# When a neighbourhood head transposes its probabilities and values: one step one half tile later, two steps one or two half tiles sooner

## The chip, the core and the metric

One core of a Trainium2 chip runs the whole program in one launch. The metric is the device time of one execution in microseconds (us). The engines are TensorE (PE in the profile; PEld is its weight load), VectorE (DVE), ScalarE (ACT), GpSimd (POOL) and SyncE (SP, which issues the transfers). The accumulators of TensorE lie in a memory of its own with eight banks, which VectorE and ScalarE read.

## The reference

Two layers of an encoder trunk work on 512 grid tokens (8 rows of 64) and 16 meta tokens, with a model width of 1024, all in float32. In each layer one projection feeds two attention branches: grouped-query attention over all tokens, and neighbourhood attention, in which a grid token sees a window of 8 rows by 16 columns with a learned bias, and the meta tokens. Cut to what matters here:

```
proj = rms_norm(x) @ w_in            # qa ka va za | qb kb vb zb | ga gb
oa   = gqa_attention(qa, ka, va) * silu(za)          # 8 heads of 64, 2 key heads
# neighbourhood attention, 8 heads of 64:
s_win  = qb . kb[window] + bias ;  s_meta = qb . kb[meta]
p      = softmax(concat(s_win, s_meta))
ob     = (p_win . vb[window] + p_meta . vb[meta]) * silu(zb)
x      = x + (sigmoid(ga) * (oa @ w_o_attn) + sigmoid(gb) * (ob @ w_o_na)) @ w_out
```

## The kernel before

**The projection is the backbone.** The input projection runs in chunks of 128 output columns, named in `project`. Each float32 product is three matmuls on two-part operands: high by high (L266), low by high (L267), high by low (L268). After about 12 matmuls over 512 tokens, or 24 over 264, `product` calls `tick()`. One such stretch is a **half tile**, about 2.9 us of TensorE's time. The weights come in 128x512 pieces: a raw transfer (`raw`), a cast by ScalarE (`whi`, L214) and a subtract by GpSimd (`wlo`, L216).

**Side work is put between the half tiles.** Both attention branches are cut into steps. A `Side` queue starts a new unit every four ticks, and each step runs a fixed number of ticks after its unit's start, as tables say: `GQA_AT` for the grouped-query units (`scores` S, transposes `pt`, meta transposes `ptm`, sums `av`), `NA_AT` for the neighbourhood heads. The two queues have starting ticks 0 and 1 of four. At one tick, the neighbourhood steps go first; the steps of the queue due at that tick go in the order of their start, a new unit last.

**A neighbourhood head** has six steps, placed by `stages`: `prepare` (loads the bias), `scores` (the score tile `Sb`, eight matmuls; VectorE adds the bias and finds the maximum, L733; ScalarE takes exponentials, L735; VectorE normalises them into `Pb`, L739), and three groups of transposes of `Pb`: `transposes1` (`ta`, and `tm` for the meta queries in layer 0), `transposes2` (`tb`), `transposes3` (`tc`); then `sums` (`avb`). `values` places three more groups for each pair of heads, which transpose the values: `vtb`, `vtc`, `vtd`, for the tile `VB2`.

**Emptying a bank.** Every transposed group goes into a bank of one pool (`ps_t`, tag `tp`) that has two banks; the next but one group needs the bank empty. ScalarE copies the high part and VectorE subtracts for the low part (`split`, L172 and L173; `split_down`, L609 and L610). The group `tb` has four such ops: two for its 128 rows, two for its 64. The score tiles `S` and `Sb` share one buffer of two banks, and the exponentials of S (`P`, L624) read it.

**Numbers used in the prediction.** A half tile is numbered by the tick count modulo 4. Heads 0 to 7 start at ticks that are 1 modulo 4, so step offset 2 is half tile 3, offset 4 is half tile 1 and offset 5 is half tile 2. The functions that the diff touches:

Of the kernel before, what the change touches and what calls it, by code (L numbers as in the profile page):

```python
# [33 lines left out]

GQA_AT = ({"scores": (0, 2), "transposes": (3, 4), "meta": 5, "sums": (5, 7)},
          {"scores": (0, 1), "transposes": (3, 6), "meta": 6, "sums": (5, 7)})
NA_AT = ({"stages": (0, 2, 5, 5, 5, 7), "values": (3, 4, 6)},
         {"stages": (0, 2, 4, 5, 5, 7), "values": (3, 4, 5)})

NORM_AT = ({"tokens": (1, 4, 6), "squares": (2, 2, 2, 3, 2), "heads": (2, 3, 5, 5, 6), "values": (1, 3)},  # L40
           {"tokens": (1, 3, 5), "squares": (2, 2, 2, 3, 2), "heads": (2, 3, 5, 5, 6), "values": (1, 3)})
# [50 lines left out]
def trunk_kernel(ctx: ExitStack, tc: tile.TileContext, xT, w, gn, bias, rope, outT):  # L92
# [255 lines left out]
    for l in range(DEPTH):  # L348
# [474 lines left out]
        def window_values(j, i):  # L823
            vb = kvq[j]["v"]
            if i == 0:
                kvq[j]["v2"] = tiny.tile([P, 6, 2, 2, HD], F32R, tag="VB2", bufs=1, name=f"VB2{l}_{j}")
                kvq[j]["o"] = slot("B", f"ob{l}_{j}")
            tiles = ([(1, 64, P), (2, 192, P), (3, 320, P)], [(4, 0, 64), (5, 448, 64)], [(0, NTOK - 32, 32)])[i]
            values(vb, kvq[j]["v2"], tiles, f"{'bcd'[i]}{l}_{j}")

        def start_head(hd):
            steps = list(zip(NA_AT[l]["stages"], windowed_head(hd)))
            if hd % 2 == 0:
                steps += [(at, lambda i=i: window_values(hd // 2, i)) for i, at in enumerate(NA_AT[l]["values"])]
            return sorted(steps, key=lambda x: x[0])
# [178 lines left out]
```

## Time and profile before

| what | value |
|---|---|
| three runs | 889.19, 889.79, 890.23 us; median 889.79 |
| the profiled execution | 890.2 us, its span 888.4 us, granted clock 0.993 |
| TensorE busy | 863.5 us, 97% of the span |
| VectorE, ScalarE, GpSimd busy | 561.6, 470.9, 356.5 us |
| neighbourhood heads of layer 0 | in the stretch 88 to 262 us |
| neighbourhood heads of layer 1 | in the stretch 517 to 700 us |

The profile is of one execution. A row of the timeline gives the start, the length, engine, line and operation, the output and inputs by the program's names, and in brackets how long the engine stood idle before it and what ended that. Matmuls overlap in these rows, so starts tell more than lengths. A row of the waits gives who waited for whom: total in us, how many times, the longest.

### The profile page before, as it was taken

Reading aid. Unit: us, or ns where it says so; the run is one execution under the profiler, and the core shown is the slowest. Engines: PE = TensorE matmul, PEld = TensorE weight load, DVE = VectorE, ACT = ScalarE, POOL = GpSimd, SP = SyncE. Lnnn points to the kernel's source line nnn. Section 1 sums busy time; section 2 is a strip of 40 time slices with the busy share of each in tenths; the row PEclk is TensorE's granted clock in tenths of the full one; section 3 lists DMA queues with packets and bytes.
Section 4 is the critical chain, followed back from the end, with each engine's and each line's share of the span. In section 5 each row is a group of like instructions: output and inputs, shape, how many; then the busy total and the mean of one; then the engine's idle time right before and its main releaser. Section 6 shows DMA issues by size and latency. Waiting matters only on the chain.

```text
span 888.4 us, 16647 instructions
## 1 busy us (share of the span) xinstructions
PE 863.5 (97%) x6208; PEld 806.4 (91%) x6208; DVE 561.6 (63%) x1285; ACT 470.9 (53%) x1045; POOL 356.5 (40%) x288
## 2 busy tenths in 40 slices
PE   8999999999999999999999999999999999999996
PEld 7988999999999999999998889988888888888896
DVE  6983777676876574336338657778867655444643
ACT  7732566666665554433445446566657554444532
POOL 5563433433223332544765544334333333345520
PEclk9998999999999999999999999999999999999998
DMA  8453343435222212324544454244421122222702
GB/s 274 114 149 100 102 126 89 128 95 134 80 73 67 66 60 84 96 84 156 185 135 125 127 161 127 78 113 137 124 79 62 59 73 72 72 83 95 262 21 76
DMA packets 51937, 96.46 MB, mean 109 GB/s; under 512 B 6544, under 2 KB 8592, under 8 KB 51856
## 3 DMA queue, kind: packets, MB, share of 16 engines
q1 hardware_dynamic: 50624, 94.33, 35.6%
q8 instruction: 49, 0.80, 0.4%
q10 hardware_dynamic: 1232, 1.06, 0.4%
q14 instruction: 32, 0.26, 0.1%
HBM read 76.20 MB, written 4.26 MB: 91 GB/s over the span
## 4 chain that ended last, share of the span: by engine, by line
PE 84%; DVE 8%; ACT 3%; DMA 2%; issue 1%; SPq 0%; POOL 0%; DVEq 0%; ACTq 0%; POOLq 0%
PE pp L266 19%; PE pp L268 19%; PE pp L267 19%; PE av L664 3%; PE pt L116 3%; PE y L266 3%; PE y L267 3%; PE y L268 3%; PE avb L797 2%; PE S L441 1%; PE S L442 1%; DVE Pb L739 1%; PE Sb L441 1%; DMA raw<-in_w_dram 1%; PE ptm L116 1%
## 5 line engine op out<-in xcount | busy, mean ns | idle before, releaser
L216 POOL TENSOR_TENSOR wlo<-raw,whi 128x512 fp32r<-128x512 f32 x216 | 290.3, 1348 | 433.7 <-ACT whi L214 384.7
L266 PE MATMUL pp<-hh,whi 128*128 128x264 f32 (+1 forms) x1056 | 335.4, 318 | 2.3 <-ACT qs L377 2.3
L268 PE MATMUL pp<-hh,wlo 128*128 128x264 f32 (+1 forms) x1056 | 330.2, 313 | 0.0
L267 PE MATMUL pp<-hl,whi 128*128 128x264 f32 (+1 forms) x1056 | 329.4, 312 | 0.0
L214 ACT CAST whi<-raw 128x512 fp32r<-128x512 f32 x216 | 132.9, 620 | 160.0 <-PE pp L267 54.5
L266 PEld LDWEIGHTS pp<-hh,whi 128*128 128x128 f32 x1056 | 199.7, 189 | 11.6 <-ACT qs L377 2.5
L268 PEld LDWEIGHTS pp<-hh,wlo 128*128 128x128 f32 x1056 | 199.9, 189 | 10.7
L267 PEld LDWEIGHTS pp<-hl,whi 128*128 128x128 f32 x1056 | 200.3, 190 | 8.9
L624 ACT ACTIVATE P<-S,st,r 128x528 f32<-128x528 f32 x64 | 50.6, 791 | 55.1 <-DVE st L623 49.4
L622 DVE TENSOR_REDUCE st<-S 128x1 f32<-128x528 f32 x64 | 45.0, 703 | 12.3 <-PE S L442 11.5
L173 DVE TENSOR_TENSOR ptl<-pt,pth 128x512 fp32r<-128x512 f32 x64 | 43.9, 687 | 13.6 <-ACT pth L172 13.1
L865 DVE TENSOR_TENSOR mg<-pp,rbc 128x264 f32<-128x264 f32 (+1 forms) x48 | 24.8, 517 | 41.6 <-PE pp L268 40.5
L172 ACT CAST pth<-pt 128x512 fp32r<-128x512 f32 x64 | 37.3, 585 | 9.7 <-PE pt L116 8.8
L116 PE MATMUL pt<-ident,P 128*128 128x128 f32 x256 | 39.5, 274 | 1.8 <-DVE VB L173 0.6
L626 DVE RECIPROCAL st<-st 128x1 f32<-128x1 f32 x64 | 10.5, 164 | 45.9 <-ACT P L624 45.4
L735 ACT ACTIVATE Pb<-Pb,stb 128x208 f32<-128x208 f32 (+1 forms) x64 | 31.0, 485 | 12.6 <-DVE stb L733 12.5
L267 PE MATMUL pp<-mxl,whi 128*128 128x264 f32 x128 | 36.7, 286 | 0.0
L268 PE MATMUL pp<-mxh,wlo 128*128 128x264 f32 x128 | 36.5, 285 | 0.0
L266 PE MATMUL pp<-mxh,whi 128*128 128x264 f32 x128 | 36.4, 285 | 0.0
L866 ACT ACTIVATE mg<-mg 128x264 f32<-128x264 f32 (+1 forms) x48 | 23.7, 493 | 22.3 <-DVE mg L865 22.1
L664 PE MATMUL av<-pth,VA 128*128 128x256 f32 x128 | 35.1, 296 | 0.0
L627 DVE TENSOR_SCALAR P<-P,st 128x528 f32<-128x528 f32 x64 | 33.6, 526 | 2.2
(616 smaller groups left out, 1848.6 us busy)
## 6 DMA issues: line engine op xcount, KB each, us to landing
raw<-in_w_dram SPq DMA_DIRECT2D x232, 256.0 KB, 2.7
bias<-in_bias_dram SPq DMA_DIRECT2D x16, 480.0 KB, 3.9
x<-in_xT_dram SPq DMA_DIRECT2D x8, 264.0 KB, 5.8
xr<-in_xT_dram SPq DMA_DIRECT2D x8, 264.0 KB, 4.5
x1d<-xr SPq DMA_DIRECT2D x8, 264.0 KB, 3.4
xf<-x1d SPq DMA_DIRECT2D x8, 256.0 KB, 5.3
KB_0l<-kb SPq DMA_DIRECT2D x8, 140.0 KB, 2.4
KB_1l<-kb SPq DMA_DIRECT2D x8, 140.0 KB, 2.4
```

The costliest lines, as they stand in the source:

```text
L116: nc.tensor.transpose(ps, src, ident[:n, :n])
L172: nc.scalar.copy(hi, src)
L173: split_at["any"] = nc.vector.tensor_sub(lo, src, hi.bitcast(F32))
L214: split_at["weights"] = nc.scalar.copy(hi, raw)
L216: sub = eng.tensor_sub(lo, raw, hi.bitcast(F32))
L266: nc.tensor.matmul(ps, wh, rh[:, a:b], start=i == 0, stop=False)
L267: nc.tensor.matmul(ps, wh, rl[:, a:b], start=False, stop=False)
L268: nc.tensor.matmul(ps, wl, rh[:, a:b], start=False, stop=i == n - 1)
L622: nc.vector.tensor_reduce(st[:n, 0:1], S[:n, :, :HALF], axis=AX.XY, op=ALU.max, negate=True)
L624: nc.scalar.activation(p[:n].rearrange("p (i k) -> p i k", i=2), S[:n, :, :HALF], AF.Exp, bias=st[:n, 1:2], scale=scale, accum_out=st[:n, ...
L627: nc.vector.tensor_scalar_mul(p[:n], p[:n], st[:n, 3:4])
L664: nc.tensor.matmul(c["av"], rows2(c["t"][i][0]), c["t"][i][1], start=i == 0, stop=i == 8)
```

## The change

Four entries of the table that places the steps of the neighbourhood heads are other numbers. In `stages` the fourth entry (`tb`) goes from 5 to 6 in both layers' terms, that is from half tile 2 to half tile 3, where the next head's `Sb` follows it. In `values` `vtd` of layer 0 goes from offset 6 to 4, and in layer 1 `vtc` from 4 to 3 and `vtd` from 5 to 4. No instruction is added or taken away, and no matmul has another shape.

```
-NA_AT = ({"stages": (0, 2, 5, 5, 5, 7), "values": (3, 4, 6)},
-         {"stages": (0, 2, 4, 5, 5, 7), "values": (3, 4, 5)})
+NA_AT = ({"stages": (0, 2, 5, 6, 5, 7), "values": (3, 4, 4)},
+         {"stages": (0, 2, 4, 6, 5, 7), "values": (3, 3, 4)})
```

In these listings a row is the line, the operation, the output and the inputs with their buffer numbers, and the shape; `ident` is the identity for a transpose and `pp` is the projection.

TensorE, layer 1, head 3. Before, `tb` and `tc` stand together at the end of a projection chunk:

```order
L268 MATMUL pp_24_0_8231<-hh_7_6415,wlo_24_1_8073 128x512
L116 MATMUL tb_3_8288<-ident,Pb_3_1_8105 128x128 x2
L116 MATMUL tb_3_8288<-ident,Pb_3_0_8104 64x128
L116 MATMUL tb_3_8288<-ident,Pb_3_1_8105 64x128
L116 MATMUL tc_3_8299<-ident,Pb_3_0_8104 32x128 x2
L116 MATMUL tc_3_8299<-ident,Pb_3_1_8105 32x128 x2
L664 MATMUL av_2_0_8306<-pth_2_0_0_8213,VA_6850 128x256
```

After, `tc` stands there alone, and `tb` comes half a tile later:

```order
L268 MATMUL pp_8_0_8327<-hh_3_6123,wlo_8_0_8222 128x512
L116 MATMUL tb_3_8340<-ident,Pb_3_1_8105 128x128 x2
L116 MATMUL tb_3_8340<-ident,Pb_3_0_8104 64x128
L116 MATMUL tb_3_8340<-ident,Pb_3_1_8105 64x128
L441 MATMUL Sb_4_8351<-KB_2h_8167,QB_2a 128x208
L442 MATMUL Sb_4_8351<-KB_2l_8174,QB_2a 128x208
```

`tb` of head 3 has moved from ahead of `tc` to directly ahead of the `Sb` of head 4.

ScalarE at the same place, before (the half tile's weight cast first):

```order
L214 CAST whi_17_1_8334<-raw_17_1_8332 128x512
L172 CAST tbh_3_8293<-tb_3_8288 128x256
L609 CAST na_120<-tc_3_8299 32x512
L586 ACTIVATE zb_2t<-zb_2_8217 128x512
L609 CAST tbh_3_8293<-tb_3_8288 64x256
L624 ACTIVATE P_2_1_1_8317,st_2_1_1_8316<-S_2_1_1_8311,st_2_1_1_8316,r_1_6912 128x528
L214 CAST whi_13_0_8454<-raw_13_0_8452 128x512
L735 ACTIVATE Pb_4_0_8353,stb_4_8352<-Pb_4_0_8353,stb_4_8352 128x208
```

And after:

```order
L214 CAST whi_17_1_8323<-raw_17_1_8321 128x512
L609 CAST na_120<-tc_3_8288 32x512
L586 ACTIVATE zb_2t<-zb_2_8217 128x512
L624 ACTIVATE P_2_1_1_8306,st_2_1_1_8305<-S_2_1_1_8300,st_2_1_1_8305,r_1_6912 128x528
L214 CAST whi_13_0_8460<-raw_13_0_8458 128x512
L172 CAST tbh_3_8345<-tb_3_8340 128x256
L609 CAST tbh_3_8345<-tb_3_8340 64x256
L735 ACTIVATE Pb_4_0_8353,stb_4_8352<-Pb_4_0_8353,stb_4_8352 128x208
```

The copies of `tb` have moved from ahead of the exponentials `P` to behind them and behind the next weight cast, directly ahead of head 4's first exponential.

VectorE at the same place, before:

```order
L173 TENSOR_TENSOR tbl_3_8294<-tb_3_8288,tbh_3_8293 128x256
L610 TENSOR_TENSOR na_120<-tc_3_8299,na_120 32x512
L622 TENSOR_REDUCE st_2_1_1_8316<-S_2_1_1_8311 128x1
L610 TENSOR_TENSOR tbh_3_8293<-tb_3_8288,tbh_3_8293 64x256
L623 TENSOR_SCALAR st_2_1_1_8316<-st_2_1_1_8316,r_1_6912 128x1
L587 SCALAR_TENSOR_TENSOR zb_2_8217<-zb_2t,zb_2_8217 128x512
```

And after:

```order
L610 TENSOR_TENSOR na_120<-tc_3_8288,na_120 32x512
L622 TENSOR_REDUCE st_2_1_1_8305<-S_2_1_1_8300 128x1
L587 SCALAR_TENSOR_TENSOR zb_2_8217<-zb_2t,zb_2_8217 128x512
L623 TENSOR_SCALAR st_2_1_1_8305<-st_2_1_1_8305,r_1_6912 128x1
L626 RECIPROCAL st_2_1_1_8305<-st_2_1_1_8305 128x1
L627 TENSOR_SCALAR P_2_1_1_8306<-P_2_1_1_8306,st_2_1_1_8305 128x528
L173 TENSOR_TENSOR tbl_3_8346<-tb_3_8340,tbh_3_8345 128x256
L610 TENSOR_TENSOR tbh_3_8345<-tb_3_8340,tbh_3_8345 64x256
L733 ISA Pb_4_0_8353,stb_4_8352<-Sb_4_8351,bias_4_8260 128x208
```

Both subtracts of `tb` have left the chain of the maximum (L622, L623) that `P` needs and stand ahead of head 4's score ops (L733); a gate multiply (L587) now stands ahead of L623.

TensorE, layer 1, head 2, before:

```order
L116 MATMUL ta_2_7979<-ident,Pb_2_0_7860 128x128 x3
L116 MATMUL ta_2_7979<-ident,Pb_2_1_7861 128x128
L565 MATMUL vtc_1_7988<-ident,vb_1_7524 64x128 x2
L441 MATMUL S_2_0_0_7996<-KA1h_7003,Q_1a 128x264
L442 MATMUL S_2_0_0_7996<-KA1l_7004,Q_1a 128x264
```

And after, where `vtc` stands one half tile ahead of this, directly behind `vtb`:

```order
L116 MATMUL ta_2_7985<-ident,Pb_2_0_7860 128x128 x3
L116 MATMUL ta_2_7985<-ident,Pb_2_1_7861 128x128
L565 MATMUL vtd_1_7994<-ident,vb_1_7524 32x128
L441 MATMUL S_2_0_0_8003<-KA1h_7003,Q_1a 128x264
L442 MATMUL S_2_0_0_8003<-KA1l_7004,Q_1a 128x264
```

`vtd` has taken the place of `vtc`; before it stood behind the next half tile's `tc`.

## Prediction

> **What bounds the kernel now.** I read the page first: busy times, slices, chain. Then TensorE's waits in the two stretches where neighbourhood heads run, and last the rows around each wait.
>
> ```profile
> span 888.4 us, 16647 instructions
> PE 863.5 (97%) x6208; PEld 806.4 (91%) x6208; DVE 561.6 (63%) x1285; ACT 470.9 (53%) x1045; POOL 356.5 (40%) x288
> PEclk9998999999999999999999999999999999999998
> ```
>
> TensorE is the bound: 97% busy at a nearly full clock. The change adds no matmul, so the time can move only through TensorE's gaps, 24.9 us in all (888.4 - 863.5). The next view gives the two stretches with heads (layer 0, layer 1) on TensorE: length, then busy time.
>
> ```profile
> 88.00:262.00 174.00, 171.29 (x1411) 166.95 (x1411) 126.17 (x380) 110.97 (x289) 60.94 (x51) 1.00 0.38 106
> 517.00:700.00 183.00, 179.61 (x1158) 158.93 (x1157) 136.96 (x336) 113.04 (x266) 64.51 (x55) 1.00 0.35 102
> ```
>
> Here the gaps are 2.71 us and 3.39 us. TensorE's waits, first in layer 0 and then in layer 1 (total, times, longest):
>
> ```profile
> PE tc L116 <- DVE tal L173: 1.1, 1, 1.1
> PE pt L116 <- DVE VB L173: 0.6, 1, 0.6
> PE pt L116 <- DVE st L623: 0.5, 1, 0.5
> ...
> PE vtd L565 <- DVE na L610: 1.4, 3, 0.8
> PE Sb L441 <- ACT P L624: 1.2, 3, 0.7
> PE vtc L565 <- DVE ptl L173: 0.5, 1, 0.5
> ```
>
> Most are of one kind: a transpose (tc, vtd, vtc, pt) waits for VectorE to finish reading what stands in its bank, since all transposes share two banks. `Sb` waits for the exponentials `P`, which read the one score tile.
>
> **The change: what it removes.** These are the waits one by one, with two neighbouring matmuls for scale (177.24, 177.36: start, length).
>
> ```profile
> 177.24 0.28 PE L266 MATMUL pp<-hh,whi 128*128 128x264 f32 x1
> 177.36 0.28 PE L267 MATMUL pp<-hl,whi 128*128 128x264 f32 x1
> 222.19 0.61 PE L116 MATMUL tc<-ident,Pb 128*32 128x128 f32 x4 [1.12 <-DVE tal L173]
> 539.30 0.29 PE L565 MATMUL vtd<-ident,vb 128*32 128x128 f32 x1 [0.24 <-DVE na L610]
> 584.93 0.41 PE L565 MATMUL vtc<-ident,vb 128*64 128x128 f32 x2 [0.53 <-DVE ptl L173]
> 591.81 0.29 PE L565 MATMUL vtd<-ident,vb 128*32 128x128 f32 x1 [0.78 <-DVE na L610]
> 613.10 0.36 PE L441 MATMUL Sb<-KB_2h,QB_2a 128*128 128x208 f32 x1 [0.74 <-ACT P L624]
> 630.26 0.28 PE L565 MATMUL vtd<-ident,vb 128*32 128x128 f32 x1 [0.38 <-DVE na L610]
> 683.89 0.37 PE L441 MATMUL Sb<-KB_3h,QB_3b 128*128 128x208 f32 x1 [0.17 <-ACT P L624]
> ```
>
> Matmuls start 0.12 us apart and last 0.28, so 0.16 of each lies over the next. A wait therefore costs its shown idle time plus 0.16.
>
> - Layer 0, head 5: `tc` came third in half tile 2, into the bank of `ta`, whose low part was late. Now `tc` comes second, into the bank of `tm`, which two short VectorE ops empty. Removed: 1.12 + 0.16 = 1.28 us.
> - Layer 1, the `vtd` behind `tc`: it moves one half tile ahead, to where `ta` stands, and `tb` no longer competes there. Removed: 0.40 + 0.94 + 0.54 = 1.88 us.
> - Layer 1, head 2: `vtc` goes directly behind `vtb` and takes the other bank. Removed: 0.53 + 0.16 = 0.69 us.
> - Layer 1, `Sb` at 613.10 and 683.89: 0.74 + 0.16 = 0.90 and 0.17; the second follows transposes, so I take it as shown. Both VectorE ops on `tb` stood among the steps that `P` waits for; they go. What is left of it is counted below as added, so gross 1.07 us.
>
> Gross removed: 1.28 + 1.88 + 0.69 + 1.07 = 4.9 us.
>
> **What it adds, layer 0.** `tb` now stands directly ahead of the next head's `Sb`, and its bank is wanted next by a `pt` (five heads) or a `ptm` (one) of the grouped-query unit. The rows of a `tb` and its evacuation, and of an `Sb` and the `pt` that follows it:
>
> ```profile
> 108.98 0.63 PE L116 MATMUL tb<-ident,Pb 128*128 128x128 f32 x4
> 109.65 0.37 ACT L172 CAST tbh<-tb 128x256 fp32r<-128x256 f32 x1 [0.68 <-PE tb L116]
> 110.22 0.41 DVE L173 TENSOR_TENSOR tbl<-tb,tbh 128x256 fp32r<-128x256 f32 x1
> 110.87 0.36 ACT L609 CAST tbh<-tb 64x256 fp32r<-64x256 f32 x1
> 111.71 0.42 DVE L610 TENSOR_TENSOR tbh<-tb,tbh 64x256 fp32r<-64x256 f32 x1
> 131.59 0.26 PE L441 MATMUL Sb<-KB_1h,QB_1a 128*128 128x208 f32 x1
> 133.25 0.38 PE L116 MATMUL pt<-ident,P 128*128 128x128 f32 x2
> ```
>
> The four evacuating ops in a row take 0.67 (109.65 - 108.98) + 0.37 + 0.41 + 0.42 = 1.87 us from `tb`'s start, about 1.95 with handovers. `pt` is wanted 0.47 (the four transposes: (0.63 - 0.28) / 3 x 4) + 1.66 (133.25 - 131.59) = 2.13 us after it. So four heads pass with nearly 0.2 us to spare. At two (heads 1 and 6) a tanh stands between the two ScalarE copies; its row, and that of a weight cast:
>
> ```profile
> 221.31 0.42 ACT L586 ACTIVATE zb_3t<-zb 128x264 f32<-128x264 f32 x1
> ...
> 612.95 0.60 ACT L214 CAST whi<-raw 128x512 fp32r<-128x512 f32 x1
> ```
>
> 1.95 + 0.42 - 2.13 is about 0.2 us each. With 0.3 for small holds at half tile 1, where `vtd` now stands among `pt` and `ptm`, layer 0 adds 0.7 us. From below it is 0 (all covered). From above each of six is held by one weight cast more: 6 x 0.60 + 0.7 = 4.3 us.
>
> **What it adds, layer 1.** Here the step ahead of `Sb` meets the exponentials of the unit's second score tile. The rows around the `Sb` of head 4 (the cast at 612.95, shown above, follows the first):
>
> ```profile
> 612.16 0.79 ACT L624 ACTIVATE P<-S,st,r 128x528 f32<-128x528 f32 x1 [1.65 <-PE pp L267]
> ...
> 614.58 0.38 PE L116 MATMUL ptm<-ident,P 128*32 128x128 f32 x2
> ```
>
> ScalarE's new order is `P`, weight cast, both copies of `tb`. The cast ends at 613.55, the copies and the last VectorE op at 613.55 + 0.37 + 0.36 + 0.42 = 614.70. `ptm`, which wants the bank, came at 614.58: held 0.12, say 0.2 us, at five heads (0, 2, 3, 4, 6): 1.0 us. Residual waits of `Sb`: the two ops taken away leave 0.83 us earlier, but a gate multiply on VectorE moves ahead of the scaled maximum that `P` needs, so I leave 0.35 us each at heads 3 and 4 and 0.2 at head 0: 0.9 us. Bounds: 0, and 5 x (0.2 + 0.60) + 1.6 = 5.6 us, if one more cast stands ahead at each and `Sb` keeps its waits.
>
> **A later cost.** The `tb` evacuation now stands ahead of the four score ops of the next head on VectorE, and so ahead of its probabilities `Pb`. Are these needed at once? The first row is head 2's normalisation, the second head 7's, the third the usual one; then the transposes `ta` that need them in heads 2 and 7.
>
> ```profile
> 581.46 2.81 DVE L739 TENSOR_SCALAR Pb<-Pb,stb 128x272 f32<-128x272 f32 x2
> 688.96 2.11 DVE L739 TENSOR_SCALAR Pb<-Pb,stb 128x208 f32<-128x208 f32 x4
> 116.71 1.11 DVE L739 TENSOR_SCALAR Pb<-Pb,stb 128x208 f32<-128x208 f32 x4
> 583.80 0.38 PE L116 MATMUL ta<-ident,Pb 128*128 128x128 f32 x2
> 690.43 0.78 PE L116 MATMUL ta<-ident,Pb 128*128 128x128 f32 x4
> 582.69 1.46 POOL L396 TENSOR_TENSOR kb<-kb,KB_2h 128x560 fp32r<-128x560 f32 x1
> 589.42 1.29 DVE L627 TENSOR_SCALAR P<-P,st 128x528 f32<-128x528 f32 x1
> 589.14 1.28 POOL L216 TENSOR_TENSOR wlo<-raw,whi 128x512 fp32r<-128x512 f32 x1 [3.35 <-ACT whi L214]
> ```
>
> In head 7 `ta` starts while the fourth multiply still runs (688.96 + 2.11 = 691.07), so a delay shows at once. In head 2 the multiplies end at 584.27 with `ta` at 583.80, and the moved `vtc` puts one more VectorE op among them. I add 0.4 us at head 7 and 0.1 at head 2, 0.5 in all; from above 0.8 (both ops) + 0.4 = 1.2 us, from below 0.
>
> These rows also price something that I can't order. Head 2's multiplies took 2.81 for two, against 1.11 for four, while GpSimd ran its subtract 582.69 to 584.15; the multiply at 589.42 took 1.29 beside GpSimd's at 589.14. These are what made `ptl` and `na` late, and so the waits of 0.69 and 0.94 us. The trace alone says that the waits go with the step that moves; 4.9 us rests on that. The Trainium skill, page "SBUF — State Buffer", section "Who interferes with whom", says that VectorE in a two-port mode and GpSimd take a shared port pair for a whole instruction, and that whoever issues first blocks the other fully. By that rule the late op can recur beside another step and the sum would be 1.6 us poorer; the trace agrees as far as these overlaps go.
>
> Everything else is moved without price: the same transposes, copies and subtracts run elsewhere under TensorE's cover; ScalarE (110.97 of 174.00, 113.04 of 183.00) has room in the mean. On the queues of SyncE and GpSimd hardly anything moves: one weight load against key moves, and the memset of a value tile ahead of one GpSimd subtract per pair, both under transfers or weights wanted half tiles later. At heads 1 and 5 of layer 1 and at each layer's last head I count no change.
>
> **Sum.** Removed 4.9; added 0.7 + 1.9 + 0.5 = 3.1, together -1.8 us. The profiled execution took 890.2, 0.4 above the median of 889.79; on it the sum gives 888.4, on the median 888.0, which I forecast. A change of 0.2% (1.8 us) is about what a measurement of this kernel can tell from no change; the forecast lies on that edge. With all added terms at nothing the gain is 4.9 us (884.9); with all at their upper bounds (4.3 + 5.6 + 1.2 = 11.1) it is a loss of 6.2 (896.0). Neither is near, since the rows give each hold at 0 to 0.4.
>
> **Rivals.**
>
> *The holds give back everything.* Eleven places (six `pt` or `ptm` in layer 0, five `ptm` in layer 1) now want the bank of `tb`. If each holds for 4.9 / 11 = 0.45 us, nothing is gained: 889.8. For: the spare times are 0.2 and -0.12, handovers could eat 0.3 more. Against: four heads' ScalarE is free there (the 0.68 idle at 109.65).
>
> *Slower, by a ScalarE queue.* One mechanism: `tb`'s copies come behind one cast more than I counted, at all eleven: 0.2 + 0.60 = 0.8 each, 8.8 - 4.9 = +3.9, so 893.7. It decides from a mean hold of 0.45 on, and is a loss by over 0.2% from 0.61. For: the cast at 612.95 does stand there in layer 1. Against: in layer 0 I see none between `tb` and `pt`.
>
> *The lock recurs.* GpSimd's subtract meets head 2's multiplies again, and `vtc` or `vtd` or `ta` waits as before: 0.69 + 0.94 = 1.63 less, so 889.5, no change. For: the two engines stay in nearly the same order. Against: the steps that waited are elsewhere.
>
> *More gain.* The small holds don't appear, only `Sb`'s rest: added 1.2, so 889.8 - 3.7 = 886.1.
>
> **How the numbers follow.** Forecast 0.47 (within a microsecond either way: 0.33 faster, 0.14 same); more gain 0.14, faster; all given back 0.15, same; lock 0.11, same (0.10) or slower (0.01); slower by the queue 0.13. So faster 0.47, same 0.39, slower 0.14. The range leaves out most of the slower case and the tail of the gain: 885.7 to 890.6.
>
> **What would show it.** Right: TensorE's waits of `vtd` for `na`, of `vtc` for `ptl` and of `tc` for `tal` are gone; new ones of at most 0.4 us of `ptm` or `pt` for `tbh` (L610) appear; `Sb` for `P` shrinks from 1.2; layer 0's idle falls by about 0.6, layer 1's by about 1.2. Wrong: waits for `tbh` near 0.8 at most heads, or `ta` waiting for `Pb` L739 over a microsecond, or matmul rows in the moved places further apart than 0.12.

## The result: 0.65% slower, and the profile after

| kernel | median, us | runs | ratio to before, with its 95% interval |
|---|---|---|---|
| before | 890.01 | 4 | |
| changed | 896.06 (895.06 to 898.15) | 4 | 1.0065 [1.0051, 1.0079] |

The forecast was 888.0, in a range of 885.7 to 890.6. The profiled execution took 895.06 us. In one execution further below, of the kernel before with `tb` in a bank of its own, the granted clock was 0.751 and the time 1048.86 us; the time and ratio given there leave it out.

The page of the changed kernel, first TensorE's totals:

```profile
span 893.2 us, 16662 instructions
PE 865.3 (97%) x6208; PEld 805.6 (90%) x6208; DVE 558.5 (63%) x1285; ACT 470.8 (53%) x1045; POOL 355.4 (40%) x288
PEclk9998999999999999999999999999999999999998
```

The gaps of TensorE are 27.9 us (893.2 - 865.3), where 24.9 were. Its busy time grew by 1.8 us (863.5 to 865.3) with no matmul added: a matmul that had to wait lies over no other, so a part of each wait (0.16 us, as in the prediction) shows as busy time. The next view takes the two stretches with neighbourhood heads, with the ends put later by the delay so far, so that they hold the same work (length, busy time of PE, PEld, DVE, ACT and POOL, granted clock, share and GB/s of the DMA):

```profile
88.00:265.00 177.00, 172.67 (x1413) 167.19 (x1413) 126.53 (x380) 111.32 (x288) 60.99 (x51) 1.00 0.36 104
520.00:706.00 186.00, 180.83 (x1164) 159.33 (x1162) 133.87 (x338) 113.55 (x269) 65.48 (x56) 1.00 0.34 100
```

Idle is 4.3 us in layer 0 (2.7 before) and 5.2 us in layer 1 (3.4 before). The clock stands at 1.00 in both, so no slower clock takes part. TensorE's waits from 88 to 706 us:

```profile
PE ptm L116 <- DVE tbh L610: 3.0, 6, 0.6
PE pt L116 <- DVE VB L173: 1.8, 2, 1.2
PE pt L116 <- DVE tbh L610: 1.3, 5, 0.4
PE Sb L441 <- DMA raw<-in_w_dram: 1.2, 2, 0.7
PE pt L116 <- DVE st L623: 0.9, 1, 0.9
PE rk L525 <- DVE pfk L490: 0.7, 1, 0.7
PE pt L116 <- DVE P L627: 0.6, 2, 0.4
PE Sb L441 <- ACT P L624: 0.6, 2, 0.3
PE tc L116 <- DVE ptl L173: 0.3, 1, 0.3
```

What the change was to take away is gone: no `vtd` waits for `na`, no `vtc` for `ptl`, no `tc` for `tal`. In their place stand eleven waits for `tbh`, the last of the four operations that empty `tb`. With 0.16 us more for each wait they cost 4.3 + 11 x 0.16 = 6.1 us. I had counted 1.4 (0.4 in layer 0, 1.0 in layer 1). Two waits of `pt` in layer 0 grew as well: for `st` from 0.5 to 0.9, and for `stm` 0.3, which no row showed before.

Why the hold is so long is to be seen at its first place in layer 0 (TensorE, ScalarE, VectorE; in brackets what ended the idle time before the row):

```profile
112.05 0.60 PE L116 MATMUL tb<-ident,Pb 128*128 128x128 f32 x4
112.69 0.37 ACT L172 CAST tbh<-tb 128x256 fp32r<-128x256 f32 x1 [0.69 <-PE tb L116]
112.65 0.43 DVE L557 TENSOR_TENSOR vb<-pp,rbc 128x264 f32<-128x264 f32 x1
113.10 0.42 DVE L173 TENSOR_TENSOR tbl<-tb,tbh 128x256 fp32r<-128x256 f32 x1
113.56 0.37 ACT L609 CAST tbh<-tb 64x256 fp32r<-64x256 f32 x1 [0.49 <-DVE tbl L173]
113.96 0.42 DVE L610 TENSOR_TENSOR tbh<-tb,tbh 64x256 fp32r<-64x256 f32 x1 [0.43 <-ACT tbh L609]
114.41 0.38 DVE L733 CUSTOM_DVE_ANT_0 Pb<-Sb,bias 128x208 f32<-128x208 f32 x1
114.52 0.63 PE L116 MATMUL pt<-ident,P 128*128 128x128 f32 x4 [0.20 <-DVE tbh L610]
```

The four operations are a strict chain across two engines: ScalarE's second copy starts 0.04 us after VectorE's first subtract ends (113.52, 113.56), having stood idle 0.49 us. From `tb`'s start to the chain's end pass 2.33 us (112.05 to 114.38). In layer 1 the same chain stands behind the exponentials and the weight cast (head 4's place):

```profile
613.94 0.79 ACT L624 ACTIVATE P<-S,st,r 128x528 f32<-128x528 f32 x1 [1.60 <-PE pp L268]
614.72 0.61 ACT L214 CAST whi<-raw 128x512 fp32r<-128x512 f32 x1
615.23 0.37 ACT L172 CAST tbh<-tb 128x256 fp32r<-128x256 f32 x1
615.63 0.42 DVE L173 TENSOR_TENSOR tbl<-tb,tbh 128x256 fp32r<-128x256 f32 x1
616.09 0.37 ACT L609 CAST tbh<-tb 64x256 fp32r<-64x256 f32 x1 [0.49 <-DVE tbl L173]
616.49 0.42 DVE L610 TENSOR_TENSOR tbh<-tb,tbh 64x256 fp32r<-64x256 f32 x1 [0.43 <-ACT tbh L609]
616.94 0.38 DVE L733 CUSTOM_DVE_ANT_0 Pb<-Sb,bias 128x208 f32<-128x208 f32 x1
617.05 0.38 PE L116 MATMUL ptm<-ident,P 128*32 128x128 f32 x2 [0.54 <-DVE tbh L610]
```

Behind the chain stands the next head's work: VectorE's first score operation (L733) comes right after the last subtract, at 114.41 and 616.94. At head 4 that is 2.07 us after the start of `Sb` (614.87); before it was 1.24 us (614.34 - 613.10).

### The profile page after: what moved, and what is told of

The parts are those of the page before. It is cut to its first block, busy times and chain, and to the rows that moved or that the text cites. A ratio compares the mean times of both kernels' runs of the same rounds, so it can differ in the third digit from the quotient of the medians.

```text
span 893.2 us, 16662 instructions
## 1 busy us (share of the span) xinstructions
PE 865.3 (97%) x6208; PEld 805.6 (90%) x6208; DVE 558.5 (63%) x1285; ACT 470.8 (53%) x1045; POOL 355.4 (40%) x288
## 4 chain that ended last, share of the span: by engine, by line
PE 79%; DVE 11%; ACT 5%; issue 2%; DMA 2%; SPq 0%; POOL 0%; DVEq 0%; ACTq 0%; POOLq 0%
PE pp L266 18%; PE pp L268 18%; PE pp L267 18%; PE av L664 3%; PE y L266 3%; PE y L267 3%; PE y L268 3%; PE pt L116 3%; PE avb L797 1%; PE S L441 1%; PE S L442 1%; ACT P L624 1%; DVE st L622 1%; PE ptm L116 1%; DVE sq L290 1%
## 5 line engine op out<-in xcount | busy, mean ns | idle before, releaser
L622 DVE TENSOR_REDUCE st<-S 128x1 f32<-128x528 f32 x64 | 45.0, 703 | 11.9 <-PE S L442 11.3
L116 PEld LDWEIGHTS pt<-ident,P 128*128 128x128 f32 x256 | 28.8, 140 | 8.5 <-issue 2.3
```

The lines of the kernel that those rows point to most:

```text
L116: nc.tensor.transpose(ps, src, ident[:n, :n])
L622: nc.vector.tensor_reduce(st[:n, 0:1], S[:n, :, :HALF], axis=AX.XY, op=ALU.max, negate=True)
```

## The experiments

Ratios are to the kernel before, measured together with each run on the same chip. "A" is the theory that `tb`'s chain holds a bank that others want.

**Half of the change each.** `tb` alone moved:

```
NA_AT = ({"stages": (0, 2, 5, 6, 5, 7), "values": (3, 4, 6)},
         {"stages": (0, 2, 4, 6, 5, 7), "values": (3, 4, 5)})
```

> Only tb is moved to half tile 3, in both layers; the values' transposes stand as before. Theory A (tb's four evacuating operations run one after the other, and hold a bank that pt or ptm wants at 11 places, 6.0 us in the profile of the changed kernel; against it stand the waits taken away): this alone carries the loss, +3 to +5.5 us against before, and ptm and pt wait for tbh some 10 times. Theory B (the loss comes from the values' transposes, which fill both banks at once and make pt wait for VB, 1.8 us, and from lateness handed on): -1 to +1 us.

Measured: 896.28 us, 1.0070 [1.0054, 1.0086]: the whole loss. Its waits for `tbh` were fewer than expected, seven: two of `pt` in layer 0 (0.7 us), and in layer 1 five of `ptm`:

```profile
PE ptm L116 <- DVE tbh L610: 4.6, 5, 1.1
```

The values' transposes alone moved, `"stages"` as before:

> Only the values' transposes are moved, in both layers; tb stands as before. Theory A: the waits of vtd for na (1.9 us) and of vtc for ptl (0.7) go, and a wait of about 1.3 us of one pt for VB comes: -2 to 0 us against before, no wait for tbh. Theory B: +2 to +5 us, with several waits for VB.

Measured: 890.6 us, 1.0008 [0.9998, 1.0018]. From its waits in layer 1:

```profile
PE Sb L441 <- ACT P L624: 2.2, 5, 0.7
PE pt L116 <- DVE VB L173: 1.2, 1, 1.2
```

The waits of `vtd` and `vtc` went here too, but `Sb` waits more often for `P` (three times and 1.2 us before), and one `pt` waits 1.2 us for `VB`, where `vtb` and `vtc` in one half tile fill both banks. So this half gives nothing, and not the -2 to 0 us that I expected. Theory B, that it carries the loss, falls with both runs.

**The layers apart.** `tb` moved in layer 0 alone, then in layer 1 alone:

> Only tb of layer 0 is moved to half tile 3. From the profile of the run with both layers' tb moved: holds of pt for tbh, Sb for P (1.1 us), less the wait of tc (1.3 us): +2 to +3 us against before.

> Only tb of layer 1 is moved to half tile 3. From the same profile: five holds of ptm, 5.4 us, less the waits of vtd for na (1.9 us) and a little: +3 to +4 us against before; with the layer 0 run together +6.4 us.

Measured: 893.29 us, 1.0042 [1.0026, 1.0058], and 892.78 us, 1.0032 [1.0020, 1.0044], against 889.18 for the kernel before: +3.7 and +2.8 by the ratios, together 6.6, like the run with both (+6.2). Layer 0 costs more than expected, layer 1 less. Two things in these profiles don't fit theory A as it stands. In layer 0 only two waits for `tbh` are listed, 0.7 us, far less than the loss; `Sb` waits 1.2 us there at head 5. And in layer 1 the waits of `vtd` for `na` go when `tb` alone moves, as they went when the values alone moved: both halves remove the same wait, so their gains don't add.

**Where the loss lies, layer by layer.** The projection's matmuls come in the same order in all these kernels, so one can be found again by its number. I take one ahead of each layer's first head and one behind its last; in the kernel before they start at 92.09 and 275.01 us, and at 512.08 and 715.02 us. The table says how much further apart the same two are in each profile. Where a layer was left as it was, the difference is still up to 0.5 us.

| profile | layer 0, us | layer 1, us |
|---|---|---|
| changed | +3.0 | +1.9 |
| `tb` alone | +2.4 | +2.3 |
| values alone | -0.1 | +0.3 |
| `tb` in layer 0 alone | +2.8 | -0.1 |
| `tb` in layer 1 alone | -0.5 | +2.3 |
| changed, both copies first (below) | +1.7 | +1.3 |
| changed, bank apart (below) | +2.7 | +0.4 |
| changed, bank apart and emptied behind the scores (below) | +0.5 | +0.3 |

**The chain made shorter.** In the changed kernel both copies come first:

```
-split(bh[:, :256], bl[:, :256], tp[:, :256])            # copy, subtract
-split_down(bh, tp[:64, 256:512], 64, 256, 512)          # copy, subtract
+with tc.high_priority():                                 # as split and split_down have it
+    nc.scalar.copy(bh[:, :256], tp[:, :256])
+    nc.scalar.copy(bh[:64, 256:512], tp[:64, 256:512])
+    nc.vector.tensor_sub(bl[:, :256], tp[:, :256], bh[:, :256].bitcast(F32))
+    nc.vector.tensor_sub(bh[64:128, 256:512], tp[:64, 256:512], bh[:64, 256:512].bitcast(F32))
```

> The changed kernel, with tb emptied in another order: both copies on ScalarE, then both subtracts on VectorE, so that the second copy no longer waits for the first subtract. Theory A: each of the 11 holds is 0.2 to 0.35 us shorter, 2.2 to 3.9 us in all, so about +2 to +4 us against before instead of +6. Theory B: no change against the changed kernel, +6 us.

Measured: 893.56 us, 1.0038 [1.0026, 1.0051], 2.4 us less than the changed kernel by the two ratios. Its rows at the place shown above:

```profile
113.24 0.38 ACT L778 CAST tbh<-tb 128x256 fp32r<-128x256 f32 x1 [0.67 <-PE tb L116]
113.51 0.37 ACT L779 CAST tbh<-tb 64x256 fp32r<-64x256 f32 x1
113.91 0.42 DVE L780 TENSOR_TENSOR tbl<-tb,tbh 128x256 fp32r<-128x256 f32 x1 [0.28 <-ACT tbh L779]
114.34 0.42 DVE L781 TENSOR_TENSOR tbh<-tb,tbh 64x256 fp32r<-64x256 f32 x1
114.91 0.30 PE L116 MATMUL pt<-ident,P 128*128 128x128 f32 x1
```

The second copy no longer waits for a subtract. `tb` started at 112.60, so the chain takes 2.16 us instead of 2.33. In all, `ptm` waits for `tbh` fell from 3.0 to 1.9 us, and no wait of `pt` for `tbh` is listed any more. As A has it. The control, the same edit in the kernel before:

> The kernel before, with the same order of copies and subtracts for tb. Theory A: there nobody waits for tb's bank to be emptied, so within 0.7 us of before. Theory B says the same; it is the control for the run with the changed kernel.

Measured: 888.21 us, 0.9981 [0.9972, 0.9991], a gain larger than expected. Since its profile explained only a part of it, I measured it again:

> The kernel before with both copies of tb ahead of its subtracts once more, with more rounds, since -1.7 us (interval 0.9972 to 0.9991) was more than its profile explains (-0.5 us from the first Sb on). Real: -1 to -2 us. Chance: within 0.7 us.

Measured: 889.02 us, 0.9994 [0.9982, 1.0006]. The gain did not come again in the times. The two profiles agree on a smaller one: by the distances of the table, both are 0.9 us shorter in layer 1, of which the idle times before TensorE's rows explain about 0.4. So a gain of this size is likely, but the times don't show it. With `vtd` of layer 0 moved as well:

> The kernel before, with both copies of tb ahead of its subtracts (which alone gave -1.7 us) and vtd of layer 0 moved as in the change, nothing else. The values' move alone took 0.7 us off the wait of tc in layer 0: about -2 us against before. If the -1.7 us was chance: -0.5 us.

Measured: 888.83 us, 0.9995 [0.9985, 1.0004]; no gain that can be told from nothing.

**The bank taken away.** The changed kernel with `tb` in another bank:

```
-tp = bank(ps_t, f"tb{nm}", "tp")
+tp = bank(ps_a, f"tb{nm}", "avn")
```

> The changed kernel, with tb written to the bank of the neighbourhood sums (avb), which is empty from the previous head's sums to this head's, instead of one of the two banks that all transposes share; the order on the engines is the same but for a few rows around the layers' last heads. Theory A (pt and ptm are held by tb's bank, 6.0 us at 11 places): all waits for tbh go, 6 us less than the changed kernel, so 0 +/- 1 us against before. Theory C (the emptying of tb only shows lateness of ScalarE and VectorE, which would then reach pt, ptm or ta another way): 1 to 3 us less than the changed kernel, +3 to +5 us against before.

Measured: 893.52 us, 1.0044 [1.0028, 1.0061]. No `pt` or `ptm` waits for `tbh` any longer, and yet only 1.9 us (by the ratios) to 2.5 us (by the medians) of the 6.1 came back. The intervals of the two runs overlap (1.0051 to 1.0061), so this size is not sure. Other waits have grown:

```profile
PE pt L116 <- DVE VB L173: 2.5, 2, 1.9
PE Sb L441 <- ACT P L624: 1.9, 4, 1.2
...
PE ta L116 <- DVE Pb L739: 0.5, 1, 0.5
```

`pt` for `VB` 2.5 (1.8 in the changed kernel), and `ta` for `Pb`, which is new. `Sb` for `P` reads 1.9 (0.6), but the waits of `Sb` put down to a transfer fell from 1.2 to 0.5, and at head 5 the same `Sb` changed its label; together they grew from 1.8 to 2.4. A wait of `tb` for `ob` (0.5) is the price of the borrowed bank. That is theory C: part of the hold only showed lateness that now appears elsewhere. The first theory, that the bank is all, falls. The table divides it: in layer 1 the bank carried 1.5 of 1.9 us, in layer 0 only 0.4 of 3.0. What is late, and through what? `tb`'s emptying still stands ahead of the next head's scores. So I put it behind them, with the bank kept apart:

```
+def empty():                              # the four operations on tb
+    split(...); split_down(...)
+side_gqa.due.setdefault(side_gqa.now + 1, []).insert(0, empty)   # heads 0 to 6
```

> The changed kernel with tb in the bank of the neighbourhood sums and, besides, its four emptying operations put behind the next head's scores (for heads 0 to 6), so that on VectorE they follow the four score operations L733 instead of standing ahead of them. Theory D (of the 6 us of holds some 3.4 us came back in the run with the bank alone, because the emptying still stands ahead of the next head's softmax): this gives back 2 to 3.5 us of what was left, so 0 to +1.5 us against before. Theory E (what is left comes from the values' transposes and the late exponentials P at Sb, which neither bank nor order touches): no change against the run with the bank alone, +3 to +4 us.

Measured: 891.68 us, 1.0023 [1.0012, 1.0033], that is +2.0 us: 1.9 us less again. By the table the gain lies in layer 0 (+2.7 to +0.5). One `pt` of its head 1, first with the bank apart, then with the emptying behind the scores too (in the kernel before it waited 0.47):

```profile
140.91 0.63 PE L116 MATMUL pt<-ident,P 128*128 128x128 f32 x4 [1.10 <-DVE st L623]
140.69 0.63 PE L116 MATMUL pt<-ident,P 128*128 128x128 f32 x4
```

VectorE at head 4's place in layer 1:

```profile
613.75 0.38 DVE L733 CUSTOM_DVE_ANT_0 Pb<-Sb,bias 128x208 f32<-128x208 f32 x1 [0.57 <-PE Sb L442]
...
615.23 0.69 DVE L173 TENSOR_TENSOR ptl<-pt,pth 128x512 fp32r<-128x512 f32 x1
615.84 0.41 DVE L173 TENSOR_TENSOR tbl<-tb,tbh 128x256 fp32r<-128x256 f32 x1
```

The score operations now wait for TensorE, 1.25 us after the start of `Sb` (612.50) as in the kernel before, and `tbl` comes behind `ptl`. The 1.9 us fall just short of what theory D expected (2 to 3.5 us given back, at most +1.5 left). The intervals of the two runs with the bank apart overlap a little (1.0028 to 1.0033), so the size is less sure than the direction. Step by step the loss goes 1.0065, 1.0044 (bank apart), 1.0023 (emptying behind the scores as well).

**The kernel before with the bank apart:**

> The kernel before with tb in the bank of the neighbourhood sums; tb stays in half tile 2. Theory A: the two shared banks serve one group fewer, so the wait of tc for tal (1.3 us) goes and those of vtd for na (1.9 us) shrink; a part comes back at Sb, as in the changed kernel (0.9 us): -1 to -3 us. Theory C: no gain, within 0.7 us.

Measured: 896.11 us, 1.0074 [1.0057, 1.0090], the opposite of what was expected. The waits that were to go did go, but `Sb` waited for `P` 12 times:

```profile
PE Sb L441 <- ACT P L624: 6.2, 12, 1.8
PE pt L116 <- DVE st L623: 2.1, 1, 2.1
```

Nearly all of the loss lies in layer 0: +4.4 us by the distances of the table, +0.2 in layer 1. There, with a bank of its own, `tb` was also put earlier on TensorE, ahead of the score tile in half tile 2, and its emptying ahead of the scaled maximum (L623) that `P` needs. So the edit changed two things, and says little of the bank alone. It fits the run above: what stands ahead of a softmax on VectorE can be paid for. With both copies first:

> The kernel before, with both copies of tb ahead of its subtracts and tb in the bank of the neighbourhood sums. If both gains stand side by side: -2.5 to -4.5 us against before; if they come from the same waits: -1.7 to -2.5 us.

Measured: 890.82 us, 1.0009 [0.9997, 1.0022]; no gain, and 5.8 us less by the ratios than without the copies' order. Why so much less stays open. No version beat the kernel before by a gain that came again.

## Why the prediction was wrong

- **What it removes: right in the main.** The waits of `tc`, `vtd` and `vtc` went, 1.28 + 1.88 + 0.69 us. That the step of `vtd` was needed for its 1.88 was wrong: they go with `tb` alone too. As counted, a part of the wait of `Sb` in layer 1 is left: at head 4 it is 0.51 us, where it was 0.74.
- **Layer 0, the hold of `pt`: wrong.** The failing step is the sum "0.67 + 0.37 + 0.41 + 0.42". It has ScalarE's second copy (0.36) run beside VectorE's first subtract. The copy waits for that subtract, so the time is 2.33 us, not 1.95. The spare time of nearly 0.2 us was in truth a lack of 0.2. The rows that I quoted could not tell: the second copy started at 110.87, after the subtract's end at 110.63, but the copy of `tc` stood on ScalarE between them. Another place of the kernel before (layer 1) had it, with ScalarE idle until the subtract ended:

```profile
590.63 0.41 DVE L173 TENSOR_TENSOR tbl<-tb,tbh 128x256 fp32r<-128x256 f32 x1
591.07 0.37 ACT L609 CAST tbh<-tb 64x256 fp32r<-64x256 f32 x1 [1.00 <-DVE tbl L173]
```

  The tanh that I priced at heads 1 and 6 (0.2 us each) shows little: the holds there are 0.25 and 0.20, and 0.20 at three of the others.
- **Layer 1, the hold of `ptm`: wrong by the same step.** The working "613.55 + 0.37 + 0.36 + 0.42" lets the second copy run beside the first subtract again. It gave 0.12 us; the five holds were 2.8 us together, with 0.16 added to each 0.72 in the mean.
- **`Sb` in layer 0: not foreseen.** The wait of `tc` at head 5 moved rather than went. The exponentials of the unit's tile start as long after `ta` as before (4.81 us, 4.65 before), but TensorE, no longer held up at `tc`, comes to the next `Sb` earlier and waits there:

```profile
225.51 0.79 ACT L624 ACTIVATE P<-S,st,r 128x528 f32<-128x528 f32 x1 [1.54 <-DVE st L623]
226.44 0.36 PE L441 MATMUL Sb<-KB_3h,QB_3a 128*128 128x208 f32 x1 [0.65 <-DMA raw<-in_w_dram]
```

  `Sb` is put down to a transfer, but starts 0.14 us after `P` ends (226.30), and needs the tile that `P` reads. That gives back 0.65 + 0.16 = 0.81 of the 1.28 us.
- **The values: a cost overlooked.** `vtc` directly behind `vtb` fills both banks, and the `pt` behind them waits until VectorE has emptied the first (624.17 + 0.56 = 624.73). I had listed the other bank as a gain only:

```profile
624.17 0.56 DVE L173 TENSOR_TENSOR VB<-vtb,VB 128x384 fp32r<-128x384 f32 x1
624.65 0.41 DVE L173 TENSOR_TENSOR VB<-vtc,VB 64x256 fp32r<-64x256 f32 x1
624.78 0.66 PE L116 MATMUL pt<-ident,P 128*128 128x128 f32 x4 [1.18 <-DVE VB L173]
```

- **The emptying ahead of the next head's softmax: right as a mechanism, too small and at the wrong place.** I gave it 0.5 us at two `ta`, and nothing to the other work of VectorE behind it. With the bank apart, putting the emptying behind the scores gave 1.9 us back, by the table in layer 0, at a `pt` that waits for `st` and an `Sb` that waits for `P`. In the changed kernel the holds of the bank stand in the list of waits in place of most of this lateness; that is read from the run with the bank apart, no run shows it by itself.
- **The sum put right.** From the forecast of -1.8 us: 6.1 instead of 1.4 for the holds is +4.7, `VB` (1.18 + 0.16) is +1.3, `Sb` in layer 0 +0.8, `st` and `stm` +0.8, and the terms that did not come (0.5 at `ta`, 0.3 of small holds, 0.2 of `Sb` in layer 1) are -1.0. That makes +4.8 us, and the table's distances +4.9. The prediction's bound with all added terms at their highest, 896.0, is near the measured 896.06 by chance: it is made of one more cast at each hold, which the rows don't show.
- **The rivals.** The slower one came nearest: it "decides from a mean hold of 0.45 on", and the eleven holds were 6.1 / 11 = 0.55 us. But its reason, one cast more ahead of the copies, is not what the rows show; and by its own sum it would have given 11 x 0.55 - 4.9 = +1.2 us, not six. The rest is what no rival had: `Sb`, `VB` and the handed-on lateness. The lock with GpSimd was not what decided: the waits that it was to bring back stayed away, and VectorE's busy time fell from 561.6 to 558.5 us. (The lock's 889.5 should read 889.6: 1.63 us off the gain of 1.8.) Long operations on VectorE still occur, as this one in the run with the emptying behind the scores (head 4, one block, 1.17 us):

```profile
618.29 1.17 DVE L739 TENSOR_SCALAR Pb<-Pb,stb 128x208 f32<-128x208 f32 x1
```

What stays open: the last 2 us of the run with bank and order apart, of which the two stretches show 0.9. Its waits (`pt` for `VB` 1.6 us, 0.6 before; `Sb` and `S` for `P` about 2, 1.5 before) are those of the values and of `P`, but no run took them away one by one.

## What to carry to other kernels

A bank is held from its first write to the end of the last operation that empties it. Where copies and subtracts alternate between two engines, add the whole chain, each length and each handover, before saying that it has time to spare; ask of each operation what its engine stood idle for. And a wait that goes because a step is moved leaves the late work late: look for who needs it next, and take a moved step's emptying as standing ahead of everything queued behind it. Two stretches with the same step can lose by different causes, so measure each by itself.

## What was not expected of the hardware

Profiles of nearly the same program differ by up to 2.7 us before the first neighbourhood head, where the programs do not differ: the matmul at 92.09 us in the kernel before starts between 90.57 and 93.31 us in these runs. After a wait of 3.6 us (`Sm` for `Q2m`) the granted clock is low for a spell that varies. From 66 to 76 us, first before, then the run with the values alone moved:

```profile
66.00:76.00 10.00, 7.29 (x39) 7.33 (x40) 4.32 (x8) 1.41 (x3) 2.43 (x3) 0.66 0.48 126
66.00:76.00 10.00, 7.33 (x50) 7.36 (x51) 4.72 (x9) 2.03 (x4) 3.60 (x4) 0.83 0.47 125
```

39 matmul records against 50 in the same time, at 0.66 and 0.83 of the clock. So a difference of a microsecond between two single profiles, as the -1.8 us of span between the kernel before and its copies-first form, is no evidence until the stretches with the edit show it; here they show 1.0 of it.
